# Splitting every second chunk of scan weights with an accumulating DMA

## The chip, the cores and the metric

The kernel runs on one core of a Trainium2 chip. The metric is the device time of one execution in microseconds (us), the median of three runs. The core has five engines that run their own instruction queues: TensorE (PE, matmuls), VectorE (DVE), ScalarE (ACT), GpSimd (POOL) and SyncE (SP, which here only issues DMAs). They wait for one another and for DMAs by semaphores. Sixteen DMA engines move the data of all queues.

## The reference

One inference step through four layers for 384 tokens: 128 of a prompt and 256 of a sample, model width 1024. Layers 0 and 3 mix the tokens with a bidirectional state-space scan (SSD), layer 1 with a short gated convolution, layer 2 with differential attention. Each layer ends in a gated conv-FFN, and each sub-layer sits between norms that are modulated by `silu(cond) @ w_mod`. The part that the change touches, cut to its core:

```python
def ssd_mixer(h, h0, w_in, conv_w, conv_b, dt_bias, a_log, d_skip, norm_g, w_out):
    z, xbc, dt_raw = jnp.split(h @ w_in, [SSM_D_INNER, SSM_D_INNER + SSM_CONV_DIM], axis=-1)
    xbc = jax.nn.silu(dwconv(xbc, conv_w) + conv_b)
    xs, bm, cm = jnp.split(xbc, [SSM_D_INNER, SSM_D_INNER + SSM_GROUPS * SSM_STATE], axis=-1)
    ...
    y_f, s_f = ssd_scan(xs, dt_f, a[0], bm, cm, h0[:, 0])
    y_b, s_b = ssd_scan(flip(xs), flip(dt_b), a[1], flip(bm), flip(cm), h0[:, 1])
    y = y_f + flip(y_b) + d_skip[:, None] * xs
    y = rmsnorm(y * jax.nn.silu(z), norm_g)
    return y @ w_out, jnp.stack([s_f, s_b], axis=1)
```

The scan works per group of four heads (8 groups) and in chunks of 128 tokens, forward and backward.

## The kernel before, in words

**Weights in two parts.** Every large product is computed with the float32r type in three passes: the weight is split into a high part (wh) and the rest (wl = weight - wh), the activation likewise (hh, hl), and PE adds wh x hh, wh x hl and wl x hh in one PSUM bank (`cm_block`, line 374). The weights come in chunks of 128 partitions x 1024 numbers, 512 KB. The whole kernel has one list of chunks (`wplan`), filled layer by layer in `plan`. `weights` hands out the next one, and `ahead` (line 140) runs in front of it. A raw chunk (wr, 4 buffers) is loaded from SP's queue at line 145. ACT rounds it into wh (line 152, 4 buffers) and DVE subtracts into wl (line 153, 4 buffers). A raw buffer is free for the next load when both have read it.

**The scans.** `ssd_core` goes over the 8 groups. A group's projection has three pairs of chunks: B and C, the two halves of x, and the gate z. Each pair holds the eight k-blocks of two output blocks, four k-blocks per chunk, so each output block reads both chunks of its pair, 24 matmuls of 384 columns. The projections of group g+1 run on PE beside the scan of group g. The scan has transposes (tp, line 701), `cbp` (line 705), states (sp, line 741), the decay matrices (ab, e and w: lines 716 to 730, on POOL, DVE and ACT) and the output (yp, line 759). POOL also scales with xw (line 740) and s (line 750). A projection's result leaves PSUM through the conv: ACT writes cv (line 430), DVE adds two taps (lines 432 and 434).

**Beside it.** The modulation of later layers is spread over the kernel in units: a 1 MB load (wm, one buffer in the scans) and 4 matmuls (modps, line 184). In the scans SP also loads ab (3 buffers), h (the initial states) and stores new states, all in one queue in order.

**What sets the order.** The program is written with a framework that replays it with its own timing and puts each engine's instructions in the order in which they came up there. So an edit changes the order of all engines. On the chip each engine keeps to its order and waits where an operand is late.

Of the kernel before, what the change touches and what calls it, by code (L numbers as in the profile page):

```python
# [10 lines left out]
F32 = mybir.dt.float32  # L11
F32R = mybir.dt.float32r
I32 = mybir.dt.int32
AF = mybir.ActivationFunctionType
ALU = mybir.AluOpType
# [29 lines left out]
class Net:  # L45
# [71 lines left out]
    def plan(self, l):  # L117

        d, j, kind = self.d, l // 3, l % 3
        out = []  # L120
        if kind == 0:
            pair = lambda g, n: self.cm_chunks(d["ssd_in"][j, g, n], 2)
            out += [(d["ssd_dt"][j], 512)] + pair(0, 0) + pair(0, 1)
            for g in range(G):
                if g + 1 < G:
                    out += pair(g + 1, 0) + pair(g + 1, 1)
                out += pair(g, 2)
            out += self.tm_chunks(d["ssd_out"][j], 16)
        elif kind == 1:
            for i in range(KB):  # L130
                out += self.cm_chunks(d["sc_in"][i], 3)
            out += self.tm_chunks(d["sc_out"], KB)
        else:
            out += [(d["qkv"][n, part, :, c * 1024:(c + 1) * 1024], 1024) for n in range(4) for part in range(3) for c in range(2)]
            out += self.tm_chunks(d["da_out"], KB)
        for i in range(NF):
            out += self.cm_chunks(d["ffn_up"][l, i], 2)
        return out + self.tm_chunks(d["ffn_down"][l], NF)

    def ahead(self):  # L140

        while len(self.raws) < min(len(self.wplan), self.wpos + WS + WR - 1):
            src, m = self.wplan[len(self.raws)]
            raw = self.wp.tile([P, 1024], F32, tag="wr", name="wr", bufs=WR)
            self.load(raw[:, :m], src)
            self.raws.append(raw)
        while len(self.parts) < min(self.limit, self.wpos + WS):
            m = self.wplan[len(self.parts)][1]
            raw = self.raws[len(self.parts)]
            hi = self.wp.tile([P, 1024], F32R, tag="wh", name="wh", bufs=WS)  # L150
            lo = self.wp.tile([P, 1024], F32R, tag="wl", name="wl", bufs=WS)
            self.S.activation(hi[:, :m], raw[:, :m], AF.Copy)  # L152
            self.V.tensor_tensor(lo[:, :m], raw[:, :m], hi[:, :m].bitcast(F32), op=ALU.subtract)  # L153
            self.parts.append((hi, lo))

    def weights(self, n):
# [902 lines left out]
```

## Time and profile before

| | |
|---|---|
| median of 3 runs | 2415.24 us (2411.56 to 2415.72) |
| the profiled execution | 2410.85 us, its span 2409.0 us |
| granted PE clock, mean | 0.975 of full speed |
| PE busy | 2291.4 us, 95% |
| DVE busy | 1613.2 us, 67% |
| ACT busy | 1248.5 us, 52% |
| POOL busy | 330.0 us, 14% |
| DMA, SP's queue | 389.52 MB, 48.8% of 16 engines |

All durations come from the one profiled execution; the median of the runs is 4.4 us longer. The first scan lies between about 80 and 345 us of the span, the second between about 1780 and 2040. The matmuls are pipelined, so the busy time of PE is not work at its peak. In lists, "idle before, releaser" says what ended the wait ahead of an instruction. Instructions that only issue a DMA are not counted as busy; on SP they appear as SPq.

### The profile page before, as it was taken

How to read it: one execution, taken by the hardware profiler on the slowest of the kernel's cores; microseconds unless marked ns; L12 is line 12 of the kernel's file. 1: busy time of each engine (PE TensorE's matmuls, PEld its weight loads, DVE VectorE, ACT ScalarE, POOL GpSimd, SP SyncE). 2: the span in 40 equal slices, each digit the busy share in tenths (PEclk: the TensorE clock that was granted, in tenths of full speed). 3: DMA queues.
4: the chain of work that ended last, by engine and by line, in shares of the span. 5: the costliest groups of instructions: out<-in, count | busy, mean ns of one | idle time of the engine just before them, and what ended most of it. 6: DMA issues, size and time to landing. Idle time of an engine off the chain costs nothing.

```text
span 2409.0 us, 35648 instructions
## 1 busy us (share of the span) xinstructions
PE 2291.4 (95%) x13132; PEld 2001.4 (83%) x13132; DVE 1613.2 (67%) x2928; ACT 1248.5 (52%) x2165; POOL 330.0 (14%) x498
## 2 busy tenths in 40 slices
PE   6989999899999999999999979999898999989998
PEld 3878887799877959998788649998687888789987
DVE  3888786677655467776645547776578888677765
ACT  3766675444453344445544444445566676554444
POOL 1222221100000010000223320000113223110000
PEclk8999999999999999999999989999999999989999
DMA  7665655533547563335434453344465654423342
GB/s 293 188 173 206 213 189 177 201 123 124 165 135 292 194 246 116 131 123 164 157 123 153 153 236 109 131 129 157 141 171 168 190 178 143 131 98 125 130 147 80
DMA packets 113375, 391.79 MB, mean 163 GB/s; under 512 B 13105, under 2 KB 25521, under 8 KB 100913
## 3 DMA queue, kind: packets, MB, share of 16 engines
q1 hardware_dynamic: 113200, 389.52, 48.8%
q8 instruction: 103, 1.69, 0.3%
q14 instruction: 72, 0.58, 0.1%
HBM read 382.39 MB, written 7.08 MB: 162 GB/s over the span
## 4 chain that ended last, share of the span: by engine, by line
PE 81%; DVE 8%; DMA 4%; issue 2%; ACT 2%; POOL 2%; SPq 0%; DVEq 0%; POOLq 0%; ACTq 0%
PE mm L374 46%; PE mm L414 20%; PE mm L846 5%; PE modps L184 3%; PE yp L414 2%; DVE e L719 2%; PE yp L759 2%; DMA wm<-in_w_mod 1%; DVE wl L153 1%; PE yp L887 1%; DVE w L723 1%; DMA h<-in_state 1%; DMA wx<-in_w_mod 1%; PE yp L374 1%; ACT jk L260 1%
## 5 line engine op out<-in xcount | busy, mean ns | idle before, releaser
L374 PE MATMUL mm<-hh,wh 128*128 128x384 f32 (+1 forms) x2352 | 795.9, 340 | 11.3 <-DVE cv L434 7.4
L374 PE MATMUL mm<-hl,wh 128*128 128x384 f32 (+1 forms) x2352 | 794.7, 338 | 1.8 <-POOL hl L346 1.8
L374 PE MATMUL mm<-hh,wl 128*128 128x384 f32 (+1 forms) x2352 | 791.5, 338 | 0.0
L153 DVE TENSOR_TENSOR wl<-wr,wh 128x1024 fp32r<-128x1024 f32 (+2 forms) x466 | 564.9, 1214 | 278.6 <-ACT wh L152 277.9
L152 ACT ACTIVATE wh<-wr 128x1024 fp32r<-128x1024 f32 (+2 forms) x466 | 483.4, 1039 | 340.7 <-PE mm L374 261.6
L374 PEld LDWEIGHTS mm<-hh,wh 128*128 128x128 f32 (+1 forms) x2352 | 442.7, 189 | 37.3 <-DVE cv L434 11.4
L374 PEld LDWEIGHTS mm<-hl,wh 128*128 128x128 f32 (+1 forms) x2352 | 442.6, 188 | 5.8 <-POOL hl L346 2.3
L374 PEld LDWEIGHTS mm<-hh,wl 128*128 128x128 f32 (+1 forms) x2352 | 442.4, 188 | 5.0 <-issue 3.1
L430 ACT ACTIVATE cv<-mm,fcw 128x384 f32<-128x384 f32 x176 | 100.1, 571 | 233.3 <-PE mm L374 228.2
L414 PE MATMUL mm<-wh,gh 128*128 128x512 f32 x528 | 208.7, 395 | 0.0
L414 PE MATMUL mm<-wl,gh 128*128 128x512 f32 x528 | 208.6, 395 | 0.0
L414 PE MATMUL mm<-wh,gl 128*128 128x512 f32 x528 | 207.9, 395 | 0.0
L432 DVE SCALAR_TENSOR_TENSOR cv<-mm,fcw,cv 128x127 f32<-128x127 f32 x352 | 144.3, 411 | 42.5 <-ACT cv L430 42.5
L439 ACT ACTIVATE gh<-fg 128x384 fp32r<-128x384 f32 x176 | 92.2, 524 | 152.5 <-PE mm L414 151.6
L268 POOL TENSOR_SCALAR m<-s 128x1 f32<-128x1 f32 x42 | 17.1, 406 | 1123.3 <-ACT jk L260 1122.4
L440 DVE TENSOR_TENSOR gl<-fg,gh 128x384 fp32r<-128x384 f32 x176 | 97.6, 557 | 96.7 <-ACT gh L439 96.1
L434 DVE SCALAR_TENSOR_TENSOR cv<-mm,fcw,cv 128x127 f32<-128x127 f32 x352 | 146.0, 416 | 10.9
L414 PEld LDWEIGHTS mm<-wh,gh 128*128 128x128 f32 x528 | 99.0, 187 | 24.7 <-issue 0.8
L414 PEld LDWEIGHTS mm<-wh,gl 128*128 128x128 f32 x528 | 99.0, 187 | 24.4
L414 PEld LDWEIGHTS mm<-wl,gh 128*128 128x128 f32 x528 | 99.0, 187 | 24.0
L184 PE MATMUL modps<-wm,sil 128*32 128x512 f32 x496 | 75.1, 646 | 13.9 <-DMA wm<-in_w_mod 12.9
L846 PE MATMUL mm<-wh,hh 128*128 128x256 f32 x288 | 83.4, 290 | 0.0
(235 smaller groups left out, 3149.7 us busy)
## 6 DMA issues: line engine op xcount, KB each, us to landing
wr<-in_ffn_up SPq DMA_DIRECT2D x176, 512.0 KB
wm<-in_w_mod SPq DMA_DIRECT2D x62, 1024.0 KB
wr<-in_ssd_in SPq DMA_DIRECT2D x96, 512.0 KB
wr<-in_ffn_down SPq DMA_DIRECT2D x88, 512.0 KB
wx<-in_w_mod SPq DMA_DIRECT2D x34, 1024.0 KB
ab<-acs SPq DMA_DIRECT2D x48, 512.0 KB
wr<-in_ssd_out SPq DMA_DIRECT2D x32, 512.0 KB
wr<-in_sc_in SPq DMA_DIRECT2D x32, 384.0 KB
```

What stands on the lines that cost most here:

```text
L152: self.S.activation(hi[:, :m], raw[:, :m], AF.Copy)
L153: self.V.tensor_tensor(lo[:, :m], raw[:, :m], hi[:, :m].bitcast(F32), op=ALU.subtract)
L184: self.PE.matmul(acc[32 * j:32 * j + 32, :], self.sil[:, kb, :], raws[:, j // 2, (j % 2) * 512:(j % 2 + 1) * 512], start=kb == 0, stop=kb ...
L374: self.PE.matmul(acc[:m], w, h, start=n == 0, stop=n == len(ops) - 1)
L414: self.PE.matmul(acc[t], g[:, o:o + n], w, start=k == 0 and i == 0, stop=k == nk - 1 and i == 2)
L430: self.S.activation(t, src, AF.Copy, scale=cw[:, 1:2])
L432: self.V.scalar_tensor_tensor(t[:, o + 1:o + n], src[:, o:o + n - 1], cw[:, 0:1], t[:, o + 1:o + n], op0=ALU.mult, op1=ALU.add)
L434: self.V.scalar_tensor_tensor(t[:, o:o + n - 1], src[:, o + 1:o + n], cw[:, 2:3], t[:, o:o + n - 1], op0=ALU.mult, op1=ALU.add)
L439: self.S.activation(hi, src, AF.Copy)
L440: self.V.tensor_sub(lo, src, hi.bitcast(F32))
L719: V.scalar_tensor_tensor(e[:, sl], abs_[t][:, 0, sl], dac[:, t, hs:hs + 1], abs_[t][:, 1, sl], op0=ALU.subtract, op1=ALU.min)
L846: PE.matmul(acc[t][:, :256], h[k][:, o:o + m], w[:, ws], start=k == 0 and i == 0, stop=k == KB - 1 and i == 2)
```

## The change

In the scans' pairs, the chunks now carry their place in the pair, 0 or 1. For a chunk with a 1 the second part is made in another way: ACT writes the negated high part into wl (`Copy` with scale -1), and a DMA issued from POOL's queue adds the raw chunk onto it in place, wl = -wh + raw. The other chunks, and all of the other stages, keep the subtraction on DVE. There are 24 such chunks in a scan, 48 in all. The raw buffer of such a chunk is free once the DMA has landed, and PE may read wl from then on.

```diff
         if kind == 0:
-            pair = lambda g, n: self.cm_chunks(d["ssd_in"][j, g, n], 2)
+            pair = lambda g, n: [c + (i,) for i, c in enumerate(self.cm_chunks(d["ssd_in"][j, g, n], 2))]
             out += [(d["ssd_dt"][j], 512)] + pair(0, 0) + pair(0, 1)
...
-            src, m = self.wplan[len(self.raws)]
+            src, m = self.wplan[len(self.raws)][:2]
...
             self.S.activation(hi[:, :m], raw[:, :m], AF.Copy)
-            self.V.tensor_tensor(lo[:, :m], raw[:, :m], hi[:, :m].bitcast(F32), op=ALU.subtract)
+            if any(self.wplan[len(self.parts)][2:]):
+                self.S.activation(lo[:, :m], hi[:, :m].bitcast(F32), AF.Copy, scale=-1.0)
+                self.GP.dma_start(lo[:, :m], raw[:, :m], accum_op=ALU.add)
+            else:
+                self.V.tensor_tensor(lo[:, :m], raw[:, :m], hi[:, :m].bitcast(F32), op=ALU.subtract)
```

The new lines shift the numbers of the later ones by four. The order of the engines' instructions changes at many places; three of them follow.

SP at the start of the first scan, before: the loads of weight chunks (wr), of the rows for the decay (ab) and of the states (h), with what each waits for.

```order
L621 DMA acs_590<-rows 32x3x128 [waits DMAHW3_49,DVE_49]
L621 DMA acs_590<-rows 32x3x128 [waits DMAHW4_49,DVE_49]
L63 DMA wm<-in_w_mod 128x2048 [waits DMAHW2_49,PE_49]
L63 DMA wr<-in_ssd_in 128x1024 [waits DMAHW6_49,DVE_49]
L63 DMA wr<-in_ssd_in 128x1024 [waits DMAHW7_49,DVE_49]
L63 DMA ab<-acs_590 128x2x512 [waits DMAHW3_49,DMAHW4_49,DMAHW0_49,PE_49]
L63 DMA ab<-acs_590 128x2x512 [waits DMAHW1_49,Pool_49]
L63 DMA ab<-acs_590 128x2x512 [waits DVE_49]
L63 DMA h_626<-in_state 128x256
```

The same place in the changed kernel; DMASW is the semaphore of a DMA issued from POOL.

```order
L625 DMA acs_593<-rows 32x3x128 [waits DMAHW3_49,DVE_49]
L63 DMA wr<-in_ssd_in 128x1024 [waits DMAHW4_49,DMAHW5_49,DMASW3_49,Activation_49]
L63 DMA wr<-in_ssd_in 128x1024 [waits DMAHW6_49,DVE_49]
L63 DMA ab<-acs_593 128x2x512 [waits DMAHW3_49,DMAHW2_49,PE_49]
L63 DMA ab<-acs_593 128x2x512 [waits DMAHW7_49,Pool_49]
L63 DMA ab<-acs_593 128x2x512 [waits DMAHW0_49,DVE_49]
L63 DMA h_629<-in_state 128x256 [waits DMAHW1_49]
L63 DMA h_631<-in_state 128x256
L63 DMA wr<-in_ssd_in 128x1024 [waits DMASW4_49,Activation_49]
```

The two wr ahead of ab both waited for DVE; now the first of them waits for an accumulating DMA (DMASW3), and the one that waits for the next accumulating DMA (DMASW4) stands behind h.

POOL at the start of the first scan, before: the parts of the activation (hl), then the scan's own xw, s and w.

```order
L346 TENSOR_TENSOR hl_250<-h_252,hh_248 128x4x128
L346 TENSOR_TENSOR hl_251<-h_269,hh_249 128x4x128
L740 TENSOR_TENSOR xw<-xt,wdt 128x256 x2
L750 TENSOR_TENSOR s<-h_626,dec 128x256
L750 TENSOR_TENSOR s<-h_628,dec 128x256
L740 TENSOR_TENSOR xw<-xt,wdt 128x256
L716 TENSOR_TENSOR w<-cb,dt 128x512 x2
```

The same place in the changed kernel, where the accumulating DMA is line 155.

```order
L155 DMA wl<-wr 128x1024
L350 TENSOR_TENSOR hl_250<-h_252,hh_248 128x4x128
L350 TENSOR_TENSOR hl_251<-h_269,hh_249 128x4x128
L155 DMA wl<-wr 128x1024 x4
L754 TENSOR_TENSOR s<-h_629,dec 128x256
L744 TENSOR_TENSOR xw<-xt,wdt 128x256 x2
L754 TENSOR_TENSOR s<-h_631,dec 128x256
L155 DMA wl<-wr 128x1024
L720 TENSOR_TENSOR w<-cb,dt 128x512 x2
```

Four accumulating DMAs now stand ahead of the first s and xw, and one ahead of the first w.

ACT in a later group of the first scan, before, from the square of a finished block (sq) to the next conv (cv).

```order
L680 ACTIVATE sq<-y_338 128x384
L565 ACTIVATE yh<-y_338,dn 128x384
L152 ACTIVATE wh<-wr 128x1024 x2
L669 ACTIVATE sz<-mm 128x384
L702 ACTIVATE xt<-tp 128x3x128 x2
L680 ACTIVATE sq<-y_339 128x384
L565 ACTIVATE yh<-y_339,dn 128x384
L430 ACTIVATE cv<-mm,cw 128x384
```

The same place in the changed kernel, where the negation is line 154.

```order
L684 ACTIVATE sq<-y_339 128x384
L569 ACTIVATE yh<-y_339,dn 128x384
L152 ACTIVATE wh<-wr 128x1024 x2
L673 ACTIVATE sz<-mm 128x384
L706 ACTIVATE xt<-tp 128x3x128 x2
L154 ACTIVATE wl<-wh 128x1024
L684 ACTIVATE sq<-y_340 128x384
L569 ACTIVATE yh<-y_340,dn 128x384
L434 ACTIVATE cv<-mm,cw 128x384
```

The negation stands three instructions behind the high parts and ahead of the next cv.

## Rows read from the trace of the kernel before

**Rows 1.** The page's slices of 60 us: busy share in tenths.
```profile
PE   6989999899999999999999979999898999989998
DVE  3888786677655467776645547776578888677765
DMA  7665655533547563335434453344465654423342
```

**Rows 2.** Busy time by window; the last columns are clock, DMA share and GB/s.
```profile
core 0: us, PE busy (x) PEld busy (x) DVE busy (x) ACT busy (x) POOL busy (x), PEclk, DMA share, GB/s
120.00:155.00 35.00, 26.56 (x180) 22.29 (x180) 28.44 (x58) 21.98 (x41) 6.85 (x7) 0.85 0.65 187
190.00:225.00 35.00, 35.00 (x236) 30.61 (x235) 31.49 (x65) 24.83 (x41) 9.70 (x11) 1.00 0.60 203
1800.00:1836.00 36.00, 26.74 (x193) 20.18 (x192) 32.45 (x69) 21.85 (x43) 14.07 (x11) 0.86 0.58 188
1872.00:1908.00 36.00, 34.83 (x235) 31.13 (x231) 31.57 (x65) 26.24 (x46) 10.77 (x11) 1.00 0.58 180
1979.00:2014.00 35.00, 34.51 (x231) 31.16 (x231) 27.92 (x59) 24.19 (x41) 10.57 (x11) 1.00 0.63 180
```

**Rows 3.** Chain of waits by line: 80 to 345 us, then 1735 to 2040 us.
```profile
by line: PE mm L374 49.8%; PE yp L759 6.8%; DVE e L719 5.6%; DMA h<-in_state 4.1%; PE modps L184 3.7%; DVE w L723 3.5%; DVE wl L153 3.4%; issue 3.0%; PE sp L741 2.8%; DMA wm<-in_w_mod 2.7%; PE tp L701 2.2%; PE cbp L705 1.5%; DVE w L724 1.3%
...
by line: PE mm L374 36.7%; DVE e L719 8.9%; DVE w L723 5.6%; DMA wm<-in_w_mod 5.3%; issue 5.2%; DVE wl L153 4.9%; DMA h<-in_state 4.3%; PE yp L759 3.9%; DVE w L724 3.3%; DVE cv L432 2.8%; PE yp L374 2.7%; DVE cv L434 2.7%; DVE cb L708 1.9%;
```

**Rows 4.** Groups by line in 40 to 345 us: busy us, mean ns, idle before.
```profile
L153 DVE TENSOR_TENSOR wl<-wr,wh 128x1024 fp32r<-128x1024 f32 x48 | 59.3, 1238 | 14.6 <-ACT wh L152 14.6
L152 ACT ACTIVATE wh<-wr 128x1024 fp32r<-128x1024 f32 x49 | 51.6, 1054 | 35.1 <-PE mm L374 29.0 <-PE yp L374 5.9
```

**Rows 5.** PE's waits, 40 to 345, then 1735 to 2040: total, times, longest.
```profile
PE yp L759 <- DVE w L724: 6.2, 2, 5.7
PE modps L184 <- DMA wm<-in_w_mod: 4.4, 2, 2.7
PE mm L374 <- DVE cv L434: 2.2, 2, 1.4
...
PE yp L759 <- DVE w L724: 6.2, 2, 5.8
PE modps L184 <- DMA wm<-in_w_mod: 4.3, 2, 2.2
PE mm L374 <- DVE cv L434: 4.0, 5, 0.8
```

**Rows 6.** Chain in a stage without a scan, and PE's timeline at two groups' cbp.
```profile
831.44 12.71 PE mm L374 x72
...
1853.51 0.83 PE L705 MATMUL cbp<-cv 128*128 128x128 f32 x6
...
1888.81 0.83 PE L705 MATMUL cbp<-cv 128*128 128x128 f32 x6
```

**Rows 7.** Chain of waits, first scan: start, us, what.
```profile
87.04 10.91 DMA h<-in_state
...
126.05 7.24 DMA wm<-in_w_mod
```

**Rows 8.** SP's timeline at the start of the first scan.
```profile
79.98 0.86 SPq L63 DMA_DIRECT2D wr<-in_ssd_in  x2
84.08 1.54 SPq L63 DMA_DIRECT2D ab<-acs  x3
```

**Rows 9.** SP's waits, 80 to 345 us.
```profile
SPq L63 <- DVE wl L153: 80.3, 26, 8.4
```

**Rows 10.** The modulation's matmuls, first scan and second: ns min, median, max.
```profile
L184 PE MATMUL modps<-wm,sil x112: 592/617/1061, 69.9 to 341.5; 128*32 128x512 f32 x112
...
L184 PE MATMUL modps<-wm,sil x72: 592/617/1061, 1761.7 to 2013.0; 128*32 128x512 f32 x72
```

**Rows 11.** ACT's timeline ahead of the first scan.
```profile
65.69 1.06 ACT L152 ACTIVATE wh<-wr 128x1024 fp32r<-128x1024 f32 x1 [1.07 <-PE yp L374]
66.66 1.03 ACT L430 ACTIVATE cv<-mm,cw 128x384 f32<-128x384 f32 x2
```

## The prediction

> **What bounds the kernel now.** I read the slices of the page first [rows 1]. TensorE (PE) shows 9 nearly everywhere, VectorE (DVE) shows 6 to 8 in the scans (slices 2 to 5 and 30 to 33) and the DMA engines 5 or 6. So PE leads, and the scans are the place where DVE is nearest to it. The windows sharpen this [rows 2]. The group from 190 us has PE busy 35.00 of 35 us at clock 1.00, DVE 31.49, ACT 24.83, DMA share 0.60. The next one is alike. The second scan leaves a little room: 34.83 of 36, and 34.51 of 35. Only the first group of each scan is different: from 120 to 155 us PE is busy 26.56 of 35 at a granted clock of 0.85, from 1800 to 1836 us 26.74 of 36 at 0.86. There DVE has 28.44 and 32.45, and PE waits for what DVE makes.
>
> Then I read the chain of waits of each scan [rows 3]. PE's matmuls hold half of the first and 37% of the second; the subtraction that the change takes away from DVE for every second chunk (wl, line 153) holds 3.4% and 4.9%. PE's own waits name its suppliers [rows 5]: DVE's w and cv for a few us, and, twice in each scan, the load of the modulation weights, wm.
>
> **What the change removes.** A scan has 24 pairs of chunks (3 for each of 8 groups), so 24 subtractions of 1.24 us go [rows 4], 30 us of DVE per scan, 59 us in both. Little of it is on the path: 3.4% of the 265 us window is 9.0 us and 4.9% of the 305 us window 14.9 us [rows 3], together 23.9 for both kinds of chunk, so about 12 for the second ones. Where the subtraction goes, PE is next, and it is full already in the groups from 190 us on [rows 2]. The most that faster DVE work can return is PE's wait for DVE, 2.2 + 6.2 + 4.0 us in the rows shown [rows 5] and another 6.2 on the same w in the second scan, 18.6 in all. The least is nothing. I take three quarters of the 12: **-9 us**.
>
> **What it adds on ACT.** 24 negations per scan. They have the form of line 152, 1.05 us [rows 4], so 25 us per scan or 3.1 us per group; ACT goes from 24.8 to 28 of 35 us [rows 2], and stays below PE. What it can hold up is the copy cv that frees a PSUM bank. PE waited 2 and 5 times for cv [rows 5]. If a negation stood ahead of each, that is 7 x 1.05 = 7.4 us; if of none, nothing. I take **+3**.
>
> **What it adds on the DMA engines.** No row shows an accumulating DMA. It must read the raw chunk and the negated part, 512 KB each, and write 512 KB. If only one read counted, the engines would hold 0.52 MB; if both, 1.05 MB. At the rate of the busy engines, 203 GB/s at a share of 0.60, so 338 GB/s [rows 2], that is 1.6 or 3.1 us of engine time. From issue to landing the nearest row is the 1 MB load of wm, 7.24 us [rows 7]; the other end is the 10.91 us of a small load behind others. I take both reads, 3.1 us of engine time, and 7.2 us to land. Three per group are 9.3 us in 35, and the share goes from 0.60 to 0.87.
>
> The Trainium skill (Collectives: The Full Stack, section on the bandwidth ceiling) says the add inside a DMA costs no time of its own, but a reduction reads two sources through one ring and so runs at half the rate of a copy. By that rule the engine time is 3.1 us and the sum below stands; without it, it would be 1.6 us, a share of 0.74, and the sum about 5 us lower. No run before the change shows it.
>
> Does the landing stay hidden from PE? 72 matmuls take 12.71 us [rows 6], 0.1765 us each. A pair has 48, 8.5 us. A group takes 35.3 us, from one cbp row to the next [rows 6], so 11.8 us per pair. wl has 4 buffers, two pairs. So the second chunk of pair p+2 can be split from the end of pair p, and is first read after 14 matmuls of pair p+2: on average 11.8 + 2.5 = 14.3 us later, at worst (no other work in pair p+1) 8.5 + 2.5 = 11.0 us. The new way to it is high part 1.05, negation 1.05, landing 7.2, and on ACT other work between the two (the sz and the two xt of the order shown in the section on the change, about 1.5): 10.8 us. It fits, barely. I cost it at **0**; with 10.91 us of landing it would be 14.5, over the worst case by 3.5 us.
>
> **What the queues do.** SP's wr loads are issued in order and wait until the raw buffer is free; SP already waits 80.3 us for wl in the first scan, 26 times [rows 9]. For half of these it now waits for the accumulate to land. Behind it stand ab, h and wm. The start of a scan has the least slack: its h loads are on the chain, with 10.91 us [rows 7]. Before, two wr went out from 79.98 and ab waited for PE until 84.08 [rows 8]. In the changed order the second of these wr stands behind h, and the first waits for an accumulate two chunks older. That chunk's high part starts at 65.69 us [rows 11]; with it (1.06), four copies (2.1), the negation (1.05) and the landing (7.2) it is there at 77.1, ahead of 84.08. So ab leaves as early as before, but the next accumulate runs beside it and h, 3.1 us of engine time. I take two thirds of that, 2 us per scan: **+4**; at least 0, at most a whole landing per scan, 14.4.
>
> The wm loads pass the same engines. A scan has 112/8 = 14 and 72/8 = 9 of their units [rows 10]. PE waited for four of them, 4.4 and 4.3 us [rows 5], so they come just in time. One that meets an accumulate is up to 3.1 us later. For the four I take 2.8 us each, **+11**; if none meets one it is 0, if all 23 do, 71.
>
> **Sum.** -9 + 3 + 0 + 4 + 11 = +9 us on the profiled execution's 2410.85: 2420. The runs' median, 2415.24, is 4.4 above that execution, so I predict **2424 us**.
>
> **Rivals.**
> Faster. The accumulate lands early, and neither the start nor wm notices. For it: the DMA engines are idle 0.4 of a group [rows 2], and ab waited for PE anyway [rows 8]. Against it: wm comes just in time. Time: 2415.24 - 9 + 3 = 2409; with the whole 12 of DVE and nothing on ACT, 2403.
>
> No change to be measured. The late wm costs what DVE returns: two of the four waits grow, 5.6, the start costs 1, so +1 and about 2416.
>
> POOL in order. The DMA waits in POOL's queue for the negation, ahead of the w and xw of the decay, which DVE and PE need. Each late negation holds POOL by about its own length, 1.05 us, three times a group, 3 us; if the decay sets every group, 16 x 3 = 48 us on the forecast: 2472. It decides from the point where the decay has less than 3 us of slack; in the second scan it nearly has (34.5 of 35 [rows 2]), in the first not. The Trainium skill (SBUF — State Buffer, section on the two separate sides) warns that a DMA issued from GpSimd waits for its descriptors while DVE runs in a two-port mode. That would make the same accumulate later; DVE's large rows here have two tensor inputs, and I give it no more weight.
>
> DMA engines as the bound. If an accumulate holds them for the whole 7.2 us, a group needs 0.60 x 35 + 3 x 7.2 = 42.7 us instead of 35. With 14 groups behind the first ones that is +108: 2523. The point is 14 / 3 = 4.7 us of engine time each. Against it: 1.05 MB at 338 GB/s is 3.1.
>
> **Chances.** Forecast, small and slower, 2416 to 2438: 0.40. Faster: 0.27. No change to be measured: 0.14. POOL: 0.11. DMA bound: 0.08. What a measurement can tell here is 0.2%, 4.8 us, so below 2410.4 counts as faster and above 2420.1 as slower; 0.08 of the forecast's 0.40 lies between. Faster 0.27, same 0.22, slower 0.51. The range goes from the best of the faster case, 2403, to POOL's price, 2472, and leaves out the DMA bound and some of the tails.
>
> **What would show it.** wl on DVE at 24 per scan instead of 48, and DVE near 28 of 35 us per group. A queue other than SP's in the list of DMA queues, with 25 MB or twice that; the DMA share of a group near 0.87. PE waits for wm grown from 4.4 and 4.3 us to about 10 each, and h of the first group landing some 2 us later. If PE waits for wl itself, the cover of 11 to 14 us was too small. If the share is near 1 in the scans, the DMA bound is right. If the first groups get shorter than 35 us and wm is no later, the faster rival is.

## The result, and the profile after

The changed kernel takes 2439.65 us (median of 4 runs, 2438.06 to 2443.37), the kernel before on the same chip 2415.15 (4 runs). The ratio is 1.0115, 95% interval 1.0102 to 1.0127: slower by 1.15%, 28 us by the ratio. (The two medians above lie 24.5 us apart; the kernel before had medians of 2411.21 to 2412.72 us beside the experiments below, with 17 to 19 runs each, and against these it is 27 to 28.) The forecast was 2424, slower, with a range from 2403 to 2472. The direction was right and the size a third of what came. The profiled execution took 2443.37 us, with a span of 2441.6, 32.6 more than the 2409.0 of the profiled execution before.

The slices and queues of the page after answer to [rows 1]. The second group of lines has packets, MB and the share of the 16 engines' span.

```profile
PE   6989999899999999999999979999888999989998
DVE  3686776577655457776555547775468677677765
DMA  8878775533537563435434453344487766423342
...
q1 hardware_dynamic: 113200, 389.52, 48.4%
q0 software_dynamic: 6912, 25.17, 5.3%
```

DVE is lighter in five of the slices 2 to 5 and 30 to 33 and the same in three, DMA is at 6 to 8 where it was 5 and 6, and PE's digits hardly move: 28 us are 1% of the span. The new queue moved 25.17 MB. Each accumulate held all 16 engines for 0.053 x 2441.6 / 48 = 2.7 us.

The windows, at the same times as in [rows 2]:

```profile
core 0: us, PE busy (x) PEld busy (x) DVE busy (x) ACT busy (x) POOL busy (x), PEclk, DMA share, GB/s
120.00:155.00 35.00, 25.16 (x172) 20.67 (x172) 25.63 (x54) 19.80 (x34) 10.71 (x12) 0.95 0.87 248
190.00:225.00 35.00, 32.78 (x213) 28.43 (x212) 26.70 (x58) 25.29 (x42) 10.93 (x13) 0.95 0.82 218
1872.00:1908.00 36.00, 33.11 (x229) 30.07 (x227) 30.13 (x59) 26.27 (x45) 14.20 (x17) 1.00 0.76 205
1979.00:2014.00 35.00, 30.73 (x199) 28.06 (x198) 22.48 (x52) 23.78 (x40) 9.83 (x12) 0.90 0.67 188
```

The full groups are no longer full: PE has 32.78 of 35 us where it had 35.00, and 30.73 where it had 34.51. DVE fell by 1.4 to 5.4 us and is not what PE waits for most. PE's own waits say what is, in 40 to 345 us and then in 1735 to 2040 [rows 5]: total, times, longest.

```profile
PE modps L188 <- DMA wm<-in_w_mod: 9.3, 4, 3.5
PE sp L745 <- POOL xw L744: 5.6, 2, 3.5
PE mm L378 <- DMA wl<-wr: 3.8, 3, 2.2
PE yp L763 <- DVE w L728: 0.9, 2, 0.5
...
PE mm L378 <- DMA wl<-wr: 12.3, 4, 4.3
PE sp L745 <- POOL xw L744: 6.4, 4, 2.8
PE modps L188 <- DMA wm<-in_w_mod: 5.2, 2, 2.8
PE yp L763 <- DVE w L728: 3.2, 2, 2.9
PE modps L188 <- DMA wx<-in_w_mod: 3.1, 1, 3.1
```

Three suppliers took DVE's place: the accumulate itself (wl<-wr, 16.1 us), the modulation weights (wm and wx, 17.6 against 8.7 before) and POOL's xw. SP waits for the accumulate too. In 80 to 345 us, against the 80.3 of [rows 9]:

```profile
SPq L63 <- DMA wl<-wr: 131.1, 19, 12.6
...
SPq L63 <- DVE wl L157: 19.0, 7, 6.8
```

One group of the second scan shows how these hang together. First the chain of waits, 1870 to 1945 us (start, us, what), then SP's timeline.

```profile
1886.44 9.07 issue
1895.53 12.42 DMA wl<-wr
1908.00 3.17 PE mm L378 x12
...
1935.39 10.81 DMA wl<-wr
...
1890.26 0.34 SPq L63 DMA_DIRECT2D wr<-in_ssd_in  x1
1890.69 0.43 SPq L63 DMA_DIRECT2D h<-in_state  x1
1891.23 0.38 SPq L63 DMA_DIRECT2D ab<-acs  x1
1891.69 0.42 SPq L63 DMA_DIRECT2D h<-in_state  x1
1892.20 0.38 SPq L63 DMA_DIRECT2D wr<-in_ssd_in  x1
1892.68 0.38 SPq L63 DMA_DIRECT2D wm<-in_w_mod  x1
1896.62 0.38 SPq L63 DMA_DIRECT2D ab<-acs  x1
1908.01 0.97 SPq L63 DMA_DIRECT2D wr<-in_ssd_in  x2
```

SP issues six loads at once from 1890.26, the time at which the accumulate issued before (at 1885.58 on POOL) lands. The next accumulate starts at 1895.53 in that burst and lands 12.42 us later; only then do PE's matmuls of this pair and SP's next wr go on, at 1908.00 and 1908.01. (The 9.07 us of "issue" are POOL, idle until ACT has made the negation.) SP held the loads back because it waits, in order, for a raw buffer that the accumulate before still read. The chain has the accumulate again from 1935.39, 10.81 us.

That a landing beside a burst is a late one shows in all 48 transfers together: the 11 for which SP issued seven or more DMAs between 6 us before and 3 us after their issue landed after 11.0 us in the median, the other 37 after 6.1. PE waited for eight transfers in the run (the seven above and one just behind the first stretch), and seven of these are among the 11. Each of the eight took 9.1 us or more, and with the median landing, 7.3, each would have been there before PE came to it.

What the waits cost is seen from the third to the last `cbp` of a scan, five groups. These are the windows of the kernel before, first scan and second, then those of the changed kernel, with the columns of the table above. The last two rows are stretches behind two of the waits for wl.

```profile
157.26:335.60 178.34, 176.14 (x1194) 156.56 (x1193) 146.84 (x301) 122.67 (x208) 52.74 (x57) 1.00 0.62 201
1853.51:2030.04 176.53, 172.50 (x1157) 155.71 (x1156) 146.59 (x301) 124.22 (x209) 52.90 (x55) 1.00 0.57 174
...
160.84:348.53 187.69, 181.05 (x1194) 158.19 (x1192) 137.40 (x288) 130.35 (x217) 60.10 (x69) 0.99 0.79 229
1873.14:2063.04 189.90, 177.58 (x1157) 163.01 (x1156) 134.75 (x287) 134.54 (x222) 60.72 (x71) 0.96 0.71 196
1946.00:1951.00 5.00, 4.76 (x21) 4.73 (x21) 0.48 (x2) 0.58 (x1) 0.00 (x0) 0.66 1.04 286
1986.00:1992.00 6.00, 5.84 (x22) 5.79 (x23) 0.82 (x2) 0.58 (x1) 0.00 (x0) 0.57 0.84 266
```

The ten groups took 22.7 us longer, of the 32.6 in all. PE was idle in them for 19.0 us instead of 6.2. Its busy time, for the same number of matmuls, grew by another 10.0, and there the granted clock is 0.99 and 0.96 instead of 1.00. In the second scan all four waits for wl, 2.5 to 4.3 us long, were followed by a stretch in which the clock was partly at the lower of its two levels, 1.2 GHz or 0.5 of full speed: 0.72 from 1908 to 1914, 0.66 and 0.57 in the two rows, and 0.57 from 2025 to 2029. The kernel before waited 0.8 us for cv at five places of these groups and kept 1.00. So a wait for wl cost more than its own length.

### The profile page after: what moved, and what is told of

Read it like the earlier page. It is cut to its first block, busy times and chain, and to the rows that moved or that the text cites. A ratio compares the mean times of both kernels' runs of the same rounds, so it can differ in the third digit from the quotient of the medians.

```text
span 2441.6 us, 35749 instructions
## 1 busy us (share of the span) xinstructions
PE 2304.4 (94%) x13132; PEld 2011.3 (82%) x13132; DVE 1572.4 (64%) x2880; ACT 1280.2 (52%) x2203; POOL 353.1 (14%) x546
## 3 DMA queue, kind: packets, MB, share of 16 engines
q0 software_dynamic: 6912, 25.17, 5.3%
## 4 chain that ended last, share of the span: by engine, by line
PE 78%; DMA 10%; DVE 5%; issue 3%; ACT 2%; POOL 2%; SPq 0%; POOLq 0%; ACTq 0%; DVEq 0%
PE mm L378 44%; PE mm L418 20%; PE mm L850 4%; DMA wl<-wr 4%; PE modps L188 3%; DMA wm<-in_w_mod 2%; PE yp L418 2%; DMA wx<-in_w_mod 2%; PE yp L763 1%; DMA h<-in_state 1%; PE yp L891 1%; DVE e L723 1%; PE sp L745 1%; DVE w L727 1%; ACT jk L264 1%
## 5 line engine op out<-in xcount | busy, mean ns | idle before, releaser
L157 DVE TENSOR_TENSOR wl<-wr,wh 128x1024 fp32r<-128x1024 f32 (+2 forms) x418 | 507.5, 1215 | 277.4 <-ACT wh L152 277.0
L188 PE MATMUL modps<-wm,sil 128*32 128x512 f32 x496 | 81.1, 662 | 22.0 <-DMA wm<-in_w_mod 20.9
L436 DVE SCALAR_TENSOR_TENSOR cv<-mm,cw,cv 128x127 f32<-128x127 f32 (+1 forms) x120 | 48.7, 407 | 64.8 <-ACT cv L434 64.7
```

What stands on the lines that cost most here:

```text
L188: self.PE.matmul(acc[32 * j:32 * j + 32, :], self.sil[:, kb, :], raws[:, j // 2, (j % 2) * 512:(j % 2 + 1) * 512], start=kb == 0, stop=kb ...
L436: self.V.scalar_tensor_tensor(t[:, o + 1:o + n], src[:, o:o + n - 1], cw[:, 0:1], t[:, o + 1:o + n], op0=ALU.mult, op1=ALU.add)
```

## The experiments

Line numbers differ between the kernels by a few. All ratios are to the kernel before on the same chip, with 95% intervals. An edit also changes the order of the instructions; two pairs keep the same order on every engine and differ by their edit alone: experiments 1 and 2, and the changed kernel and experiment 6.

**1. The transfer left out.** The DMA's line is taken out; the negation stays.

```diff
-                self.GP.dma_start(lo[:, :m], raw[:, :m], accum_op=ALU.add)
```

> The accumulating DMA is left out: the 48 second parts stay the negated high part (the sum is not formed), ACT's 48 negations stay, DVE's 48 subtractions stay away. Landing theory (the DMA's time to land delays SP's next loads and PE): all of the loss goes and what DVE gives back is seen, 2405 to 2412 us. Volume theory (the DMA engines are shared): the same. ACT theory (the negations make ACT late): the loss stays, 2430 or more.

Measured: 2393.33 us, 0.9929 (0.9914 to 0.9944). PE's waits of 1735 to 2040 us:

```profile
PE yp L762 <- DVE w L727: 5.0, 2, 4.8
PE sp L744 <- POOL xw L743: 2.4, 2, 1.4
PE yp L762 <- DVE ab L733: 0.5, 1, 0.5
PE modps L187 <- DMA wm<-in_w_mod: 0.4, 1, 0.4
```

What the change takes from DVE is worth 17 us with the negations already paid, not the 6 of the forecast (-9 and +3). The transfer thus costs 45, from 0.9929 to 1.0115. And the wait for wm is gone (0.3 us in the first scan). A part of it had probably come from raw buffers that DVE freed late: with the buffers free early and DVE's work as before (experiment 10) it is 4.5 us in both stretches, against 8.7.

**2. POOL's place in the order.** POOL makes one column in place of the DMA, with the same wait.

```diff
-                self.GP.dma_start(lo[:, :m], raw[:, :m], accum_op=ALU.add)
+                self.GP.tensor_scalar(lo[:, :1], lo[:, :1].bitcast(F32), 1.0, 0.0, op0=ALU.mult, op1=ALU.add)
```

> In place of the accumulating DMA stands a POOL instruction on one column of the second part (the sum is not formed); it waits in POOL's queue for the negation as the DMA did, and PE waits for it, but nothing is moved. POOL theory: most of the loss stays, 2428 or more. Landing and volume theories: as without the DMA, 2405 to 2413 us.

Measured: 2395.68, 0.994 (0.9925 to 0.9955), within 3 us of experiment 1, which the intervals don't tell from nothing. That POOL waits for the negation ahead of w and xw costs little, and most of the loss is not there.

**3. An eighth of the transfer.** Only 128 of the 1024 columns are added.

```diff
-                self.GP.dma_start(lo[:, :m], raw[:, :m], accum_op=ALU.add)
+                self.GP.dma_start(lo[:, :128], raw[:, :128], accum_op=ALU.add)
```

> The accumulating DMA moves only 128 of 1024 columns (the other seven eighths of each second part stay negated), all waits stay. Volume theory: nearly all of the loss goes, 2408 to 2415 us. Landing theory: a small DMA still has to be issued by POOL and to land, I expect 2.5 to 4 us instead of 7.3, raw buffers are held that long, so a third to a half of the loss stays, 2417 to 2427. POOL theory (POOL's queue is held by the wait for the negation): all of the loss stays, about 2438.

Measured: 2407.91, 0.9986 (0.9974 to 0.9998). The time is that of the volume theory; neither a third of the loss nor all of it stayed. But with 3.15 MB and 1.1% of the engines it still costs 14 us over experiment 1. PE never waited for wl in the two stretches, but 7.5 us for wm in the first and 6.6 for wx and wm in the second.

**4. From device memory.** The accumulate adds the same rows, read from device memory; ScalarE's rounding frees the raw buffer.

```diff
-                self.GP.dma_start(lo[:, :m], raw[:, :m], accum_op=ALU.add)
+                self.GP.dma_start(lo[:, :m], self.wplan[len(self.parts)][0], accum_op=ALU.add)
```

> The accumulating DMA adds the same rows from HBM and not from the raw buffer, so the raw buffer is free as soon as ACT has read it and SP's queue never waits for the accumulate; volume per DMA and PE's wait for it stay. Queue theory (SP's loads, stuck behind the buffer that the accumulate holds, go out in a burst and late): more than half of the loss goes, 2415 to 2425 us, and the landings lose their long ones (10 us and more). Volume theory: the loss stays or grows, 2436 to 2450, since the engines now also read 25 MB more from HBM.

Measured: 2417.11, 1.002 (1.0006 to 1.0035). The same 25.17 MB, 5.8% of the engines, a median landing of 7.6 us. The time is that of the queue theory. SP no longer waits for it, and the longest landing is 11.1 instead of 13.1, though landings over 10 us were to go altogether. Half of the 45 us (23) thus goes with the hold of the raw buffer, as far as the other source and the shifted order cost nothing; the other half stays. PE's waits of 1735 to 2040 us:

```profile
PE modps L188 <- DMA wm<-in_w_mod: 5.5, 2, 3.4
PE mm L378 <- DMA wl<-in_ssd_in: 5.0, 4, 1.9
PE yp L763 <- DVE w L728: 4.3, 2, 4.0
```

**5. An eighth, from device memory.**

```diff
-                self.GP.dma_start(lo[:, :m], raw[:, :m], accum_op=ALU.add)
+                self.GP.dma_start(lo[:, :128], self.wplan[len(self.parts)][0][:, :128], accum_op=ALU.add)
```

> As the version that adds from device memory, but only 128 of the 1024 columns are added; the other columns of the low part stay the negated first part. The raw buffer is free as soon as ScalarE has negated... no later than in the version without the DMA. Theory 1 (of the eighth-size DMA's 14 us over the version without it, the hold of the raw buffer until landing is the larger part): 2393 to 2401 us, 0.993 to 0.996 of before. Rival (the fixed landing time of even a small DMA makes PE wait): as the eighth-size DMA, 2405 to 2411, with PE waiting for the DMA at the low part's matmuls.

Measured: 2405.52, 0.9973 (0.9963 to 0.9984): the rival's time, but not by its wait. Holding the raw buffer costs 3 us (0.9986 to 0.9973) when the transfer is small, which the intervals don't tell from nothing, and 23 when it is full. How long SP waits doesn't tell that cost: it waited 208.0 us in experiment 3 and 291.9 in the changed kernel. The 11 us that even this transfer costs over experiment 1 came as waits for wm and wx (7.1 us, then 6.8), not for wl. They lie at the starts of the scans: from the third to the last `cbp` PE was busy without a break (178.46 and 169.07 us). Why such a small transfer makes wm late, or whether the shifted order does, stays open.

**6. A plain copy.** The same bytes from and to the same places, without the addition.

```diff
-                self.GP.dma_start(lo[:, :m], raw[:, :m], accum_op=ALU.add)
+                self.GP.dma_start(lo[:, :m].bitcast(F32), raw[:, :m])
```

> The changed kernel with each accumulating DMA made a plain copy of the same 512 KB from the raw buffer to the low part (which then holds the chunk itself instead of its second part). If an accumulating transfer costs the DMA engines more than a copy of the same bytes, its packets take near half of the 5.3% of the engines' time, it lands in 3 to 5 us instead of 7.3, and the kernel comes out between the eighth-size accumulate and the full one, 2410 to 2425 us. If addition costs the engines nothing, 2432 to 2446, as the changed kernel.

Measured: 2411.93, 1.0002 (0.9989 to 1.0015). This run tells most. The queue's row and the landings (minimum, median, maximum) of the copy, the landings of the changed kernel, and the copy's windows from the third to the last `cbp` of each scan:

```profile
q0 software_dynamic: 6912, 25.17, 2.6%
...
DMA to landing us min/median/max: 2.8/5.0/10.6
...
DMA to landing us min/median/max: 4.5/7.3/13.1
...
158.38:338.06 179.68, 178.67 (x1194) 156.65 (x1193) 135.47 (x287) 130.39 (x217) 53.70 (x69) 1.00 0.73 244
1860.25:2031.87 171.62, 169.78 (x1158) 156.11 (x1157) 132.79 (x287) 134.61 (x222) 55.22 (x71) 1.00 0.67 223
```

2.6% against 5.3%: a copy holds the engines for 0.026 x 2409.8 / 48 = 1.3 us, the accumulate for 2.7, twice as long, and it lands 2.3 us later in the median. PE waits 2.8 us for wl in both stretches together instead of 16.1, SP 216.8 in the whole run instead of 291.9. The addition alone costs 27 us (1.0002 to 1.0115). As all instructions and their order are the same, nothing else can. The two profiled executions differ by 31.8 us, and 26.3 of these lie in the ten groups of the windows: 16.1 us of PE's idle time, nearly all of it waits for wl (13.2) and wm (2.8), and 10.2 us of longer matmuls at a clock of 0.99 and 0.96 instead of 1.00.

**7. From the raw buffer, with nobody waiting.** The low part stays negated; the transfer goes to 48 scratch tiles in device memory.

```diff
+        self.nscr = 0
...
-                self.GP.dma_start(lo[:, :m], raw[:, :m], accum_op=ALU.add)
+                scr = self.dp.tile([P, 1024], F32, name=f"scr{self.nscr}")
+                self.nscr += 1
+                self.GP.dma_start(scr[:, :m], raw[:, :m], accum_op=ALU.add)
```

> As the run before it, but the scratch tiles get their rows from the raw buffer, which is held until the DMA has landed; no matmul waits for the DMA. If holding the raw buffer costs what the step from the version from device memory to the changed kernel suggests, some 22 us above the run before it, so 2412 to 2442 by theory 1 or 2 of that run, and SP waits at L63 for the DMA 150 us or more in the run; if PE's wait for a late low part is what the hold turned into, within 6 us of the run before it.

Measured: 2423.79, 1.0053 (1.0032 to 1.0073). The run that it was to be held against (experiment 8) gave nothing, so it is read against the others: 30 us above experiment 1 with no matmul behind the transfer, 15 us (1.0053 to 1.0115) below the changed kernel. That is near the 16.1 us in which PE waited for wl there, but the comparison isn't clean, since this transfer starts when the chunk has landed and not after the negation, its target is device memory, and SP waited only 17.7 us for it, not the 150 that were expected.

**8. From device memory to device memory.** As 7, with the source of 4.

```diff
-                self.GP.dma_start(scr[:, :m], raw[:, :m], accum_op=ALU.add)
+                self.GP.dma_start(scr[:, :m], self.wplan[len(self.parts)][0], accum_op=ALU.add)
```

> The version without the accumulate onto the low part (which stays the negated first part), plus 48 accumulating DMAs of the same rows from device memory onto 48 scratch tiles in device memory: the volume, with no raw buffer held and no matmul that waits. Theory 1 (the 24 us that the version from device memory lost against the one without the DMA are PE's wait for the low part and the waits that this passes on): 2392 to 2402 us. Theory 2 (they are the shared DMA engines, which make wm and the chunks land late): 2408 to 2420, with PE's wait for wm near 8 and 5 us again.

Measured: 2512.12, 1.0422 (1.0407 to 1.0438), outside both theories, and it says nothing on them. These transfers wait for nothing in the kernel, so POOL issued many of them ahead of the first stage. PE's longest wait of 40 to 345 us shows it:

```profile
PE mm L331 <- DVE xn L288: 65.0, 1, 65.0
```

**9. Beside the kernel before.** VectorE subtracts everywhere; 48 accumulates of the raw buffer onto one scratch tile are added.

```diff
+        self.scr = self.dp.tile([P, 1024], F32, name="scr")
...
+            self.V.tensor_tensor(lo[:, :m], raw[:, :m], hi[:, :m].bitcast(F32), op=ALU.subtract)
             if any(self.wplan[len(self.parts)][2:]):
-                self.S.activation(lo[:, :m], hi[:, :m].bitcast(F32), AF.Copy, scale=-1.0)
-                self.GP.dma_start(lo[:, :m], raw[:, :m], accum_op=ALU.add)
-            else:
-                self.V.tensor_tensor(lo[:, :m], raw[:, :m], hi[:, :m].bitcast(F32), op=ALU.subtract)
+                self.GP.dma_start(self.scr, raw[:, :m], accum_op=ALU.add)
```

> The kernel before, with VectorE subtracting for all chunks and no negation, and with 48 accumulating DMAs added that put the same 512 KB of the raw buffer onto a scratch tile in device memory that nothing reads. No matmul depends on them; each still keeps its raw buffer until it has landed. Theory 1 (the raw buffers are held, SP's loads for later stand behind that, and the rows of wm and xw come late): 2430 to 2445 us, with SP waiting at L63 for this DMA some 200 us or more in the run and PE waiting for wm near the 8 to 9 us of the changed kernel's first scan. Rival (only PE's wait for the low part itself costs time): within 7 us of the kernel before, 2408 to 2418. Had the share of the DMA engines alone decided, it would lie with the version that adds from device memory, 1.002 of before, whose raw buffers were free early.

Measured: 2459.33, 1.0194 (1.017 to 1.0219), above theory 1 and not by its cause. SP waited 11.4 us for this DMA, not 200. POOL waited instead, with its later work behind it: 262.6 us until chunks had landed from which it was to add, and 29.6 since all wrote the same tile. PE then waited for POOL's xw. What POOL's accumulates waited for (first two lines), and PE's wait of 40 to 345 us:

```profile
  DMA wr<-in_ssd_in: 262.6, 38
  DMA scr<-wr: 29.6, 5
...
PE sp L744 <- POOL xw L743: 12.3, 6, 3.3
```

It shows that such transfers can cost 47 us where no matmul reads them. How much of that is POOL's wait for the chunks and how much the one tile stays open.

**10. The raw buffer free early, VectorE as before.**

```diff
-                self.S.activation(lo[:, :m], hi[:, :m].bitcast(F32), AF.Copy, scale=-1.0)
-                self.GP.dma_start(lo[:, :m], raw[:, :m], accum_op=ALU.add)
+                self.V.tensor_tensor(lo[:, :m], hi[:, :m].bitcast(F32), hi[:, :m].bitcast(F32), op=ALU.subtract)
```

> The kernel before, but for the second chunk of each pair VectorE subtracts the first part from itself, so the second part is zero and the raw buffer is free after ScalarE's rounding; VectorE's work is unchanged. Theory A (the version without the DMA gained 18 us mainly from raw buffers that come free earlier): 2394 to 2403 us. Theory B (it gained them from VectorE's 1.4 us less for each of these chunks): 2408 to 2415, the time of before.

Measured: 2407.39, 0.9984 (0.9975 to 0.9993). Theory B, and 4 us of A: if the two add up, of experiment 1's 17 us some 4 are the raw buffer and 13 are VectorE's work (1.24 us for each chunk by [rows 4], not 1.4).

**11. POOL subtracts.**

```diff
-                self.S.activation(lo[:, :m], hi[:, :m].bitcast(F32), AF.Copy, scale=-1.0)
-                self.GP.dma_start(lo[:, :m], raw[:, :m], accum_op=ALU.add)
+                self.GP.tensor_tensor(lo[:, :m], raw[:, :m], hi[:, :m].bitcast(F32), op=ALU.subtract)
```

> The second chunk of each pair has its low part made by one subtraction on POOL, in place of the negation and the DMA. If the relief of VectorE and of SP's queue is what the version without the DMA gained (0.993 of before), and POOL has room for three more operations in a group of 35 us, 2393 to 2410 us; if POOL's xw and its own copies are pushed late by some 4 us each, or POOL and VectorE slow one another, 2415 to 2440 with PE's waits for POOL xw above the 3.6 and 2.4 us of the version without the DMA.

Measured: 2434.28, 1.0096 (1.0081 to 1.011). POOL had the room, and PE waited 1.0 and 1.4 us for its xw, no more than in experiment 1. But DVE paid for it, and in 1735 to 2040 us PE waited 15.2 us for DVE's cv and 7.2 for its w. POOL's new operation, then two of DVE's in 40 to 2100 us, with POOL's subtractions and in the changed kernel (busy us, mean ns, idle before):

```profile
L154 POOL TENSOR_TENSOR wl<-wr,wh 128x1024 fp32r<-128x1024 f32 x48 | 128.8, 2683 | 216.1 <-ACT wh L152 215.7
...
L722 DVE SCALAR_TENSOR_TENSOR e<-ab,dac 128x128 f32<-128x128 f32 x192 | 101.8, 594 | 0.0
L678 DVE TENSOR_TENSOR y<-y,sz 128x384 f32<-128x384 f32 x32 | 37.6, 1179 | 14.2 <-ACT sz L672 14.0
...
L723 DVE SCALAR_TENSOR_TENSOR e<-ab,dac 128x128 f32<-128x128 f32 x192 | 75.3, 453 | 6.7 <-DMA ab<-acs 6.7
L679 DVE TENSOR_TENSOR y<-y,sz 128x384 f32<-128x384 f32 x32 | 19.3, 608 | 22.8 <-ACT sz L673 22.7
```

The same operations took 594 instead of 453 ns and 1179 instead of 608; DVE was busy 1637.0 us in all, against 1572.4 for the same number of instructions. What moved to POOL came back as longer operations on DVE.

**12. One chunk of three, from device memory.** Only the third pair of a group is split by the accumulate.

```diff
-            pair = lambda g, n: [c + (i,) for i, c in enumerate(...)]
+            pair = lambda g, n: [c + (i * (n == 2),) for i, c in enumerate(...)]
...
-                self.GP.dma_start(lo[:, :m], raw[:, :m], accum_op=ALU.add)
+                self.GP.dma_start(lo[:, :m], self.wplan[len(self.parts)][0], accum_op=ALU.add)
```

> Only the second chunk of each group's third pair is split by ScalarE's negation and an accumulate, which reads device memory; VectorE subtracts for the others. Each of the three chunks of a group is worth a third of the gain without a DMA (18 us) and a third of the loss from device memory (24 us) if both add up: 2411 to 2415, no change. If only the pairs whose landing meets a burst of loads cost something, and this one lies outside it, 2402 to 2409, and this would be faster than before and after.

Measured: 2410.47, 0.9996 (0.9985 to 1.0006): no change, as if gain and cost add up. No version with the whole computation beat the kernel before.

## Why the prediction was right in sign and short in size

Read as steps, from each experiment to the next by its ratio: DVE relieved and negations paid, -17; POOL's place, +3; a copy of the bytes, +15; the addition in it, +27. The sum, +28, must agree with the result, since the steps only divide it; what each is worth is what the runs add. The +3 is within the noise, and the +15 contains a shift of the order as well; the +27 is the addition alone.

- **DVE, -9, and ACT, +3.** Together -17 was measured. The forecast took a share of the chain for wl alone. The bound beside it, PE's waits for DVE of 18.6 us, was the better guide: in experiment 1 the same waits, for w and cv, are 7.5 (2.5 and 5.0 for w, none for cv), and the wait for wm, which no one had put down to DVE, went from 8.7 to 0.7. Against that PE's wait for xw grew from 2.7 to 6.0. That is 16 of the 17.
- **The landing of wl, 0.** This is the step that failed. The chain of 10.8 us against a cover of 11.0 to 14.3 "fits, barely" with 7.2 us to land, and 7.3 is the median. The cover was read rightly: at the median no transfer would have kept PE waiting. But the median didn't decide. Landings went to 13.1 us beside SP's bursts, and the working had priced that end: with 10.91 us the way is 14.5, over the cover by 3.5. PE's longest waits for wl were 2.2 and 4.3, 16.1 us in seven, and what the lower clock behind them took came on top, which no term of the forecast had. Where cover and chain differ by 0.2 us at the near end, the term isn't 0.
- **What the queues do.** It was seen that SP waits for the accumulate ahead of ab, h and wm, but the price was set for the start of the scans alone, +4. The h loads at the start landed after 11.12 us in the first scan and 14.94 in the second, against 10.91 [rows 7] and 13.13: +0.2 and +1.8, near the 2 us that were expected of each. The starts as a whole cost more: 3.6 us up to the third cbp of the first scan (157.26 to 160.84), and another 6.7 from the last cbp of that scan to the third of the second. But most of the loss lies in the later groups. From the third to the last cbp, five groups in each scan, it took 187.69 and 189.90 us where it had taken 178.34 and 176.53: 22.7 of the 32.6 us between the profiled executions. There the held loads go out as a burst and the next accumulate meets them.
- **wm, +11.** 17.6 against 8.7 before: +9. Right in size, but that was partly luck. The forecast let wm meet 3.1 us of engine time; with an eighth of the bytes, and no buffer held, PE waited 13.9 us for wm and wx (experiment 5). Against experiment 1, where DVE's relief had removed this wait, the change has +17.
- **Two reads.** The forecast chose both reads and 3.1 us of engine time; 2.7 was measured, and 1.3 for a copy. The rule of the Trainium skill (Collectives: The Full Stack, section on the bandwidth ceiling), that the add has no time of its own but reading two sources halves the rate, agrees with this trace in its size, 2.6% to 5.3% of the engines for the same bytes. What was mis-sized is the difference that this makes: "about 5 us" in the prediction, 27 in the runs, since a transfer twice as long is late at PE, first of all for wl, and the clock fell behind these waits (experiment 6).
- **The DMA share, 0.87.** 0.87 in the first group, 0.82, 0.76 and 0.67 in full ones, which also last longer. The engines were not the bound: 2.7 us is below the 4.7 of that rival.
- **POOL in order.** This rival falls: experiment 2 gives +3, within the noise.
- **No change, faster.** Both needed an accumulate that lands early. Experiment 6 is near that case, with the copy and its median of 5.0 us: 1.0002, no change.

What stays open: what part of the 15 us of a copy is bandwidth and what is order, since an eighth of the bytes costs 11 to 14 us over experiment 1; and how much of that part lies in xw, for which PE waited 6.0 us in experiment 1, 10.2 with the copy and 12.0 in the changed kernel.

## What to carry to other kernels

A DMA that takes an operation from an engine brings its landing into two chains: that of whoever reads the result, and that of the queue that waits for its source buffer. Compare the cover with the longest landings beside the busiest loads, not with a median, and where the cover is short by that measure, price the whole difference, and look at PE's granted clock behind such a wait. Ask first what the relief is worth with the transfer left out, since that is the most that it can return.

## What the runs showed of the hardware

An accumulating DMA within the core's own memory holds the DMA engines twice as long as a copy of the same 512 KB (2.7 and 1.3 us), and POOL's instruction that issues it took 872 ns in the mean, against 576 for the copy. The same accumulate with its rows in device memory lands as fast in the median (7.6 and 7.3 us). A subtraction of 128x1024 on POOL took 2683 ns, and some DVE operations that ran in the same stages became up to 1.9 times as long in the mean (608 to 1179 ns). The Trainium skill (SBUF — State Buffer, section on the two separate sides) speaks of a port that the two engines share; that DVE lost with POOL's large operations agrees with it. Its other warning, that a DMA issued from GpSimd waits for its descriptors while DVE runs in a two-port mode, no run here shows.
